# Identity made in place, and other places for transposes and value loads in a hybrid attention layer

## Chip, core and metric

The kernel runs on one core of one Trainium2 chip. Its time is the device time of one execution in microseconds. The program is one launch that computes the whole layer for two request groups.

## What is computed

One encoder layer with two parallel attentions, for two sequences (prompt and sample) of 2048 tokens and width 1024, all in fp32:

```python
h = rms_norm(x, norm_w)
q_a, k_a, v_a, g_a, q_b, k_b, v_b, g_b = jnp.split(h @ w_in, IN_SPLITS, axis=-1)
o_a = windowed_gqa_sink(rope(norm(q_a)), rope(norm(k_a)), v_a, sink_a) * jax.nn.silu(g_a)
o_b = neighbourhood_attn(norm(q_b), norm(k_b), v_b, rpb_b) * jax.nn.silu(g_b)
x = x + jnp.concatenate([o_a, o_b], axis=-1) @ w_out
out = x + (p @ w_ple) * jax.nn.sigmoid(x @ w_ple_gate)
```

The first attention has 8 query heads and 2 key heads and sees 128 tokens to each side. The second has 8 heads; it takes the tokens as a grid of 32 rows by 64 columns, and each token sees 8 rows by 16 columns around it, with a learned bias by relative position. The softmax of the second attention is over all keys that a query sees.

## The kernel before

**Products in split halves.** An fp32 operand is split into a high half (a cast to fp32r by ScalarE, ACT) and a low half (raw minus high, by VectorE, DVE). A product is then the sum of three fp32r products (high by high, high by low, low by high); `project` issues them, 8 blocks of 128 rows, so 24 matmuls for one output of 128 tokens by 512 columns.

**Units and filler.** The work is counted in tiles of 128 tokens, f from 0 to 95. f 0 to 31 are the first attention; f 32 to 95 are the second: 32 tiles for heads 0 to 3, then 32 for heads 4 to 7. A unit of the second attention (`unit_b`) takes one tile of queries, 8 grid rows by 16 columns, and a window of keys of 12 or 15 rows by 24 or 32 columns. The keys are cut into 3 or 4 chunks of at most 128 (`chunks`); 4 where the window is 15 rows by 32 columns. While a unit runs, TensorE also works through a stream of filler: the projections of later tiles (`proj_a`, `proj_b`) and, at the end, the first products of the gate branch (`ple_ahead`: pple, evicted as ev and stored to ple_d). The tables `PLAN_A` and `PLAN_B` say when each act of a unit comes, as a share of the tile's filler (the first number): all four "sc", then "exp", "prep" (the next unit's queries), "pt" and "po"; the entries with 0 in second place belong to the unit before ("po" 2 and 3, "fin"). A tile of filler is 10320, counted as 48 matmuls of 215 each; in the last units (`TAIL`) it is 8100. Whether a unit takes the one or the other table is decided in the last loop of `emit`.

**The acts of a unit of the second attention.** "sc" h makes the scores of head h in PSUM (scb) and VectorE adds the bias into s, with the row maximum (line 277); "exp" are four exponentials on ACT (line 301, order of heads 0, 2, 1, 3), which begin as soon as the maximum is negated into nm (line 295). "pt" x transposes the weights of the x-th head of that order to ptb, chunk by chunk; ACT and VectorE split it into p_t (lines 941 and 942). "po" x multiplies p_t by the values vw (pob); "fin" multiplies by the gate (o_tb) and stores to ob_d (line 970).

**Two kinds of units.** In most units, those for which `copied_(f)` is true (all but f 55 to 58 and 87 to 95, so 51 of 64), ACT also issues a DMA after each exponential that copies s, as it is, to a tile tn of type fp32r (line 310); the first copy goes out behind the second exponential, the second behind the third, the last two behind the fourth. Their transposes read tn and are line 262 in the trace. In the other 13 units, called fp32 units below, s is transposed itself (line 264).

**Value loads.** `load_values` issues the loads of vw, one for each chunk, on SP's queue (line 907). In a copied unit they are made to wait for one of the last four exponentials: `last_ex[1]`, which is the unit's second. SP's queue is in order, and most transfers stand on it: the blocks of x (stx), bias, the stores v_d and ob_d, and the reloads of split weights.

**Who sets the order.** TensorE's order is the program's, by dependencies that `pinned` adds. On the other engines a scheduler places instructions by when it takes their inputs to be ready, save those pinned with `P`. The queues run in the order in which they were placed. PSUM has buffers of three tags: "pj" (3, projections), "sc" (3, scores and transposes), "ms" (2, pob and others).

**The start.** The identity is made by GpSimd in a small pool of its own (`eye_`), cast by VectorE to `ident` and, with its columns in another order, by GpSimd to `rowwise`. The pool is closed at once, so its memory may be given to tiles that come later. Then come eight warm-up matmuls (pwarm), the loads of x blocks (stx) and weights (ws, wg), their splits (wx for keys and values of the first attention, wa for queries, wb for gates), and the first products: pk for tiles 0 and 1, then pq for both, then pg.

Of the kernel before, what the change touches and what calls it, by code (L numbers as in the profile page):

```python
# [11 lines left out]
F32 = mybir.dt.float32  # L12
F32R = mybir.dt.float32r
# [6 lines left out]
NT = SEQ // 128  # L20
# [38 lines left out]
def bias_offsets():  # L59
# [33 lines left out]
PLAN_A = (  # L93
    (0.04, 1, "sc", 0), (0.10, 1, "sc", 1), (0.12, 1, "sc", 2), (0.12, 1, "rest", 0), (0.14, 1, "sc", 3),
    (0.14, 1, "rest", 1), (0.14, 0, "po", 0),
    (0.22, 0, "po", 1), (0.34, 0, "po", 2), (0.45, 0, "fin", 0), (0.46, 1, "prep", 0), (0.58, 1, "den", 0),
    (0.75, 1, "pt", 0), (0.79, 1, "pt", 1), (0.88, 1, "pt", 2),
)
PLAN_B = (
    (0.00, 1, "sc", 0), (0.03, 1, "sc", 1), (0.07, 1, "sc", 2), (0.09, 0, "po", 2), (0.11, 1, "sc", 3), (0.16, 0, "po", 3),  # L100
    (0.16, 1, "exp", 0), (0.24, 0, "fin", 0), (0.35, 1, "prep", 0),
    (0.60, 1, "pt", 0), (0.68, 1, "pt", 1), (0.76, 1, "pt", 2), (0.91, 1, "po", 0), (0.94, 1, "pt", 3), (0.98, 1, "po", 1),
)


def emit(ctx, tc, io):
    nc = tc.nc
    dram = ctx.enter_context(tc.tile_pool(name="dram", bufs=1, space=bass.MemoryType.DRAM))
    cp = ctx.enter_context(tc.tile_pool(name="const", bufs=1))
# [3 lines left out]
        tag = PSM.get(tag, tag)  # L113
        return pp.tile(shape, F32, tag=tag, name=name, bufs=PSB[tag])

    ident, rowwise = (cp.tile([128, 128], F32R, tag=n, name=n) for n in ("ident", "rowwise"))
    with tc.tile_pool(name="eye", bufs=1) as ep:
        eye_ = ep.tile([128, 128], F32, tag="eye", name="eye")
        make_identity(nc, eye_)
        nc.vector.tensor_copy(ident, eye_)  # L120
        nc.gpsimd.tensor_copy(rowwise.rearrange("p (r c) -> p r c", c=16), eye_.rearrange("p (c r) -> p r c", r=8))
    nw = cp.tile([128, KT], F32, tag="nw", name="nw")
    nc.scalar.dma_start(nw, io["norm_w"])
    ms_a = cp.tile([128, 2 * NT], F32, tag="ms_a", name="ms_a")
# [159 lines left out]
    last_ex = []  # L284

    def after(ins, other):

        tc.add_manual_dep(ins.ins, other.name, mybir.DependencyInfo(mybir.DependencyClass.Sync, mybir.DependencyReason.DATA),
                          reason="behind the copies")
# [486 lines left out]
    def keys_b(kt, b, cb):  # L776
        pkt = ptile([128, 2, 16, 8], "ms", "pktb")
        for i in range(2):
            tr(pkt[:, i].rearrange("p c r -> p (c r)"), kt[:, 2 * i:2 * i + 2, :].rearrange("p h d -> p (h d)"))
        for e in range(2):  # L780
            a, z = 64 * e, 64 - 64 * e
            hi, lo = (ks_b[e][p:p + 64, 8 * b:8 * b + 8, :, 16 * cb:16 * cb + 16].rearrange("p r i c -> p i c r")
                      for p in (a, z))
            nc.scalar.copy(hi, pkt[a:a + 64])
            nc.vector.tensor_tensor(out=lo, in0=pkt[a:a + 64], in1=hi.bitcast(F32), op=ALU.subtract)
# [85 lines left out]

    bt = []

    def copied_(f):

        return not (4 * NT - 9 <= f < 4 * NT - 5 or f >= 6 * NT - 9)

    def unit_b(f):
        half, st = divmod(f - 2 * NT, 2 * NT)
        s, j = divmod(st, NT)  # L880
# [5 lines left out]
        n = nr * ncol  # L886
        if cb != 2:
            off, _ = BIAS_OFF[(row_type(b), col_type(cb))]
            if not bt:
                bt.append(big([128, 2, 4, 512], F32, "bias"))  # L890
            bt.append(bt[0][:, len(bt) % 2])
            load = nc.sync.dma_start(bt[-1][:, :, :n],
                                     io["bias"][half][:, off:off + 4 * n].rearrange("p (h n) -> p h n", h=4))
            if f > 2 * NT and copied_(f) and copied_(f - 1):
                after(load, last_ex[-1])
# [3 lines left out]
        def load_values():  # L899

            spare = f >= 6 * NT - 6 and f % 2 == 0
            if spare:
                four = ap.tile([128, 4, 4, 2 * HD], F32R, tag="raw", name="vw4", bufs=1)
            for j in range(nch):
                v = four[:, j] if spare else \
                    ap.tile([128, 4, 2 * HD], F32R, tag=("vp", "vr_")[j % 2], name="vw", bufs=3 - j % 2)
                load = nc.sync.dma_start(v[:kn[j]].bitcast(F32).rearrange("p h d -> p (h d)"),
                                         v_d[half, s, cb][r0 + ch[j][0]:r0 + sum(ch[j])]
                                         .rearrange("r c h a d -> (r c) (h a d)"))
                if copied_(f):  # L910
                    after(load, last_ex[1])
                vw.append(v)

        sees = [query_rows(b, cb, j) for j in range(nch)]
# [4 lines left out]
        def sc(h):  # L919
            ps = ptile([128, 512], "sc", "scb")  # L920
            for j, q in enumerate(qs[f]):
                mm(ps[:, :n].rearrange("p (r c) -> p r c", c=ncol), q[h % 2][:, 128 * (h // 2):128 * (h // 2) + 128],
                   ks_b[h % 2][:, r0:r0 + nr, h // 2, c0:c0 + ncol], j == 0, j == 1)
            softmax(h, ps, n, bias[:, h, :n], sm)
            if h == 3:
                if not tn:
                    tn.append(ap.tile([128, 4, 480], F32R, tag="ev", name="tn", bufs=1))
                got["ex"] = exps(sm, hr_b[:, st:st + 1], gs, turned=tn[0] if copied_(f) else None)
                next(got["ex"])
# [33 lines left out]
        def fin(_):  # L963
            pgt = ptile([128, 2, 128], "sc", "pgtb")
            for i in range(2):
# [4 lines left out]
            nc.sync.dma_start(ob_d[s][b, :, 2 * half:2 * half + 2, cb, :], o_t)  # L970
        return {"sc": sc, "pt": pt, "po": po, "fin": fin, "prep": lambda _: nxt(f),
                "exp": lambda _: (next(got["ex"]), load_values())}


# [106 lines left out]
    def drain(gen, count=10 ** 9):  # L1081
        for _ in range(count):
            if next(gen, None) is None:
                return
# [49 lines left out]
    for f in range(6 * NT):  # L1134
        in_a = f < 2 * NT
        while done < f + (2 if in_a else 6) and done < 6 * NT:
            drain(stream, 48 - owed)
            owed = 0
            done += 1
        total = 13008 if done < 2 * NT - 1 else 15480 if done < 2 * NT else 10320 if done < 6 * NT else TAIL  # L1140
        done += 1
        spent = 0
        for kv in range(2 if in_a else 1):
            unit = unit_a(f, kv) if in_a else unit_b(f)
            for part, now, act, i in PLAN_A if in_a else PLAN_B:
                at = (kv + part) / (2 if in_a else 1)
                while spent < at * total:
                    spent += next(stream, total)
                if now or prev:
                    (unit if now else prev)[act](i)  # L1150
            prev = unit
        while spent < total:
            spent += next(stream, total)
        if f in (2 * NT - 1, 6 * NT - 1):
            for part, now, act, i in PLAN_A if in_a else PLAN_B:
                if not now:
                    if f == 6 * NT - 1:
                        drain(stream, 4)
                    prev[act](i)
            prev = None  # L1160
        if f == 2 * NT - 1:
            for p in pending:
                drain(stream, 8)
                keys_b(*p)
            owed = 16
# [4 lines left out]
    with tc.tile_pool(name="c", bufs=1, reuse_waits="tile") as op:  # L1170
# [208 lines left out]
        for m in range(7 * len(groups)):  # L1379
            n, i = divmod(m, 7)  # L1380
# [94 lines left out]
```

## Time and profile before

| what | value |
|---|---|
| median of 3 runs | 2485.05 us (2482.97 to 2488.8) |
| profiled execution, its own time | 2484.0 us |
| its span, first to last instruction | 2482.2 us |
| mean granted clock of TensorE | 0.997 |
| TensorE busy | 2445.7 us (99%) |
| VectorE / ACT / GpSimd busy | 1699.0 / 1411.2 / 851.0 us |
| moved by DMA | 479.65 MB, mean 193 GB/s |

In rows of a timeline the first number is the start in us, the second the length; a row can stand for several instructions (x3), and the bracket tells how long the engine was idle before it and what ended that. PE is TensorE, PEld its weight loads, SPq and ACTq are the DMA issues of SP and ACT. In rows of waits the numbers are the total in us, how many times, and the longest. The profiled execution lies 1.05 us under the median, and 1.8 us of its time lie outside the span.

### The profile page before, as it was taken

Reading aid. Unit: us, or ns where it says so; the run is one execution under the profiler, and the core shown is the slowest. Engines: PE = TensorE matmul, PEld = TensorE weight load, DVE = VectorE, ACT = ScalarE, POOL = GpSimd, SP = SyncE. Lnnn points to the kernel's source line nnn. Section 1 sums busy time; section 2 is a strip of 40 time slices with the busy share of each in tenths; the row PEclk is TensorE's granted clock in tenths of the full one; section 3 lists DMA queues with packets and bytes.
Section 4 is the critical chain, followed back from the end, with each engine's and each line's share of the span. In section 5 each row is a group of like instructions: output and inputs, shape, how many; then the busy total and the mean of one; then the engine's idle time right before and its main releaser. Section 6 shows DMA issues by size and latency. Waiting matters only on the chain. (4 is left out here: it accounts for less than half of the span.)

```text
span 2482.2 us, 40847 instructions
## 1 busy us (share of the span) xinstructions
PE 2445.7 (99%) x13062; PEld 2063.1 (83%) x13062; DVE 1699.0 (68%) x4215; ACT 1411.2 (57%) x3408; POOL 851.0 (34%) x1363
## 2 busy tenths in 40 slices
PE   8999999999999999999999999999999999999999
PEld 7888888888888888887888788888788888888887
DVE  6877777777775666666666666666537655687776
ACT  6777777776754655665656566665663222344443
POOL 4555555555543544454544444443110000000000
PEclk9999999999999999999999999999999999999999
DMA  6422232322354667667966687778867455756765
GB/s 208 137 95 94 88 103 95 100 94 88 103 179 131 219 231 240 232 211 248 304 201 227 223 263 252 245 249 273 289 229 274 163 169 174 269 174 215 243 227 170
DMA packets 275255, 479.65 MB, mean 193 GB/s; under 512 B 31168, under 2 KB 116064, under 8 KB 270816
## 3 DMA queue, kind: packets, MB, share of 16 engines
q1 hardware_dynamic: 245376, 437.84, 53.4%
q10 hardware_dynamic: 29664, 39.19, 4.7%
q8 instruction: 104, 1.70, 0.3%
q14 instruction: 111, 0.91, 0.1%
HBM read 307.72 MB, written 134.23 MB: 178 GB/s over the span
## 5 line engine op out<-in xcount | busy, mean ns | idle before, releaser
L258 PE MATMUL pvg<-wb,xr 128*128 128x512 f32 x1536 | 447.8, 404 | 0.4 <-DMA wb<-sp_1wb 0.3
L258 PE MATMUL pqk<-wa,xr 128*128 128x512 f32 x1536 | 442.7, 411 | 0.0
L301 ACT ACTIVATE s<-s,nm 128x320 f32<-128x320 f32 (+6 forms) x512 | 293.2, 574 | 150.0 <-DVE nm L298 118.6
L258 PEld LDWEIGHTS pvg<-wb,xr 128*128 128x128 f32 x1536 | 270.4, 189 | 34.9 <-DMA wb<-sp_1wb 1.3
L258 PEld LDWEIGHTS pqk<-wa,xr 128*128 128x128 f32 x1536 | 262.1, 189 | 35.0
L1260 ACT CAST opd<-raw 128x512 fp32r<-128x512 f32 x224 | 131.5, 619 | 271.3 <-PE acca L1278 118.2
L379 POOL TENSOR_TENSOR xr<-stx,xr 128x512 fp32r<-128x512 f32 x186 | 237.6, 1293 | 117.4 <-ACT xr L378 91.3
L1261 DVE TENSOR_TENSOR opd<-raw,opd 128x512 fp32r<-128x512 f32 x224 | 146.5, 686 | 147.2 <-ACT opd L1260 147.2
L258 PE MATMUL pg<-wb,xr 128*128 128x512 f32 x768 | 233.1, 409 | 1.0 <-DVE vv L536 1.0
L258 PE MATMUL pq<-wa,xr 128*128 128x512 f32 x768 | 219.4, 400 | 0.0
L942 DVE TENSOR_TENSOR p_t<-ptb,p_t 128x368 fp32r<-128x368 f32 (+5 forms) x256 | 119.4, 486 | 125.9 <-ACT p_t L941 124.6
L941 ACT CAST p_t<-ptb 128x368 fp32r<-128x368 f32 (+5 forms) x256 | 106.8, 426 | 123.4 <-PE ptb L262 79.0
L1278 PE MATMUL accc<-opd,wb 128*128 128x512 f32 x768 | 176.7, 389 | 0.0
L1278 PE MATMUL acca<-opd,wa 128*128 128x512 f32 (+1 forms) x780 | 175.9, 386 | 0.5 <-ACT r L1356 0.5
L1278 PE MATMUL acca<-opd,s 128*128 128x512 f32 x768 | 175.4, 389 | 0.0
L1278 PEld LDWEIGHTS acca<-opd,wa 128*128 128x128 f32 x780 | 145.0, 188 | 30.2 <-ACT r L1356 0.7
L1278 PEld LDWEIGHTS accc<-opd,wb 128*128 128x128 f32 x768 | 144.2, 188 | 29.9
L1278 PEld LDWEIGHTS acca<-opd,s 128*128 128x128 f32 x768 | 144.2, 188 | 29.9
L960 ACT COPY otb<-pob 64x512 f32<-64x512 f32 x128 | 74.3, 581 | 160.1 <-PE pob L258 158.3
L143 POOL TENSOR_TENSOR yb<-vrb,power 128x8 f32<-128x8 f32 x64 | 106.4, 1662 | 148.7 <-DVE vrb L813 148.7
L258 PEld LDWEIGHTS pob<-p_t,vw 128*128 128x128 f32 (+2 forms) x832 | 134.2, 189 | 21.4 <-DVE p_t L942 1.5
L258 PEld LDWEIGHTS pq<-wa,xr 128*128 128x128 f32 x768 | 135.1, 189 | 17.3
(174 smaller groups left out, 5188.0 us busy)
## 6 DMA issues: line engine op xcount, KB each, us to landing
stx<-x_b SPq DMA_DIRECT2D x128, 256.0 KB
vw<-v_d SPq DMA_DIRECT2D x96, 256.0 KB
stx<-x_a SPq DMA_DIRECT2D x64, 256.0 KB
stn<-x_n SPq DMA_DIRECT2D x64, 256.0 KB
v_d<-vb SPq DMA_DIRECT2D x64, 256.0 KB
ple_d<-ev SPq DMA_DIRECT2D x64, 256.0 KB
xres<-x_r SPq DMA_DIRECT2D x64, 256.0 KB
x_d<-r SPq DMA_DIRECT2D x64, 256.0 KB
```

Source lines behind the costliest of these rows:

```text
L143: nc.gpsimd.tensor_tensor(out=y, in0=v, in1=power.broadcast_to([128, n]), op=ALU.pow)
L258: pinned(nc.tensor.matmul(out, lhsT, rhs, start=start, stop=stop))
L301: ex = nc.scalar.activation(ss[i], ss[i], AF.Exp, bias=nm[:, i:i + 1], accum_out=den[:, i:i + 1])
L379: low.tensor_tensor(out=lo, in0=raw, in1=hi.bitcast(F32), op=ALU.subtract)
L941: nc.scalar.copy(hi, pf)
L942: nc.vector.tensor_tensor(out=lo, in0=pf, in1=hi.bitcast(F32), op=ALU.subtract)
L960: nc.scalar.copy(ot[a:a + 64], pq[z:z + 64])
L1260: P(nc.scalar.copy(hi, v))
L1261: P(nc.vector.tensor_tensor(out=lo, in0=v, in1=hi.bitcast(F32), op=ALU.subtract))
L1278: pinned(nc.tensor.matmul(ps[:, cols], w[k][:, a, c:c + 128], o[:, b, cols], start=i in (0, 1, 4) and k == 0 and j == 0, stop=k == 3 and j ...
```

## The change

Three things change. The identity is made in `ident` itself, an fp32 tile, with no pool of its own and no cast; only `rowwise` is still a copy. `copied_` moves to the top and the fp32 units take `PLAN_B` with "pt" and "po" at 0.45 to 0.80 of the tile, the copied units a table `PLAN_C` of their own at 0.60 to 0.98. The value loads of copied units wait for `last_ex[2]`, the unit's third exponential.

```diff
 PLAN_B = (
     (0.00, 1, "sc", 0), ..., (0.16, 1, "exp", 0), (0.24, 0, "fin", 0), (0.35, 1, "prep", 0),
-    (0.60, 1, "pt", 0), (0.68, 1, "pt", 1), (0.76, 1, "pt", 2), (0.91, 1, "po", 0), (0.94, 1, "pt", 3), (0.98, 1, "po", 1),
+    (0.45, 1, "pt", 0), (0.52, 1, "pt", 1), (0.60, 1, "pt", 2), (0.66, 1, "po", 0), (0.74, 1, "pt", 3), (0.80, 1, "po", 1),
 )
+PLAN_C = (
+    (0.00, 1, "sc", 0), ..., (0.16, 1, "exp", 0), (0.24, 0, "fin", 0), (0.35, 1, "prep", 0),
+    (0.60, 1, "pt", 0), (0.70, 1, "pt", 1), (0.80, 1, "pt", 2), (0.92, 1, "po", 0), (0.95, 1, "pt", 3), (0.98, 1, "po", 1),
+)
+def copied_(f):
+
+    return 2 * NT <= f and not (4 * NT - 9 <= f < 4 * NT - 5 or f >= 6 * NT - 9)
...
-    ident, rowwise = (cp.tile([128, 128], F32R, tag=n, name=n) for n in ("ident", "rowwise"))
-    with tc.tile_pool(name="eye", bufs=1) as ep:
-        eye_ = ep.tile([128, 128], F32, tag="eye", name="eye")
-        make_identity(nc, eye_)
-        nc.vector.tensor_copy(ident, eye_)
-        nc.gpsimd.tensor_copy(rowwise.rearrange("p (r c) -> p r c", c=16), eye_.rearrange("p (c r) -> p r c", r=8))
+    ident = cp.tile([128, 128], F32, tag="ident", name="ident")
+    make_identity(nc, ident)
+
+    rowwise = cp.tile([128, 128], F32R, tag="rowwise", name="rowwise")
+    nc.gpsimd.tensor_copy(rowwise.rearrange("p (r c) -> p r c", c=16), ident.rearrange("p (c r) -> p r c", r=8))
...
                 if copied_(f):
-                    after(load, last_ex[1])
+                    after(load, last_ex[2])
...
-            for part, now, act, i in PLAN_A if in_a else PLAN_B:
+            for part, now, act, i in PLAN_A if in_a else PLAN_C if copied_(f) else PLAN_B:
```

What moves is seen in the engines' orders. First SP's queue at the very start of the program (stx are blocks of x, ws and wg raw weights: 128x2x256 those of pk, 128x2x512 those of pq; rw and snk_all are small tables), before:

```order
L238 DMA ws<-w_in 128x2x512 x2
L238 DMA wg<-w_in 128x512 x4
L433 DMA rw<-rope_w 128x64
L455 DMA snk_all<-sink 128x8
L361 DMA stx<-x_a 128x512
L238 DMA ws<-w_in 128x2x256
L361 DMA stx<-x_a 128x512
L238 DMA ws<-w_in 128x2x256 x3
```

and now:

```order
L370 DMA stx<-x_a 128x512
L247 DMA ws<-w_in 128x2x256
L370 DMA stx<-x_a 128x512
L247 DMA ws<-w_in 128x2x256 x3
L370 DMA stx<-x_a 128x512 x2
L247 DMA ws<-w_in 128x2x512 x4
L370 DMA stn<-x_n 128x512 x2
L247 DMA wg<-w_in 128x512 x4
L440 DMA cs<-rope 128x512
L442 DMA rw<-rope_w 128x64
L370 DMA stn<-x_n 128x512 x2
L464 DMA snk_all<-sink 128x8
```

The first block of x moves from the ninth transfer to the first, and the weights of pq and pg and the small tables go behind. VectorE's order there moves in the same way, before:

```order
L405 MEMSET warm 128x512
L120 CAST ident<-eye 128x128
L458 COPY snk<-snk_all 64x8 x2
L471 TENSOR_SCALAR snk<-snk 128x8
L158 SCALAR_TENSOR_TENSOR wa_113<-ws,nw,wa_113 128x512
```

and now:

```order
L414 MEMSET warm 128x512
L388 TENSOR_TENSOR xr<-stx,xr 128x512
L167 SCALAR_TENSOR_TENSOR wx<-ws,nw,wx 128x256 x2
L388 TENSOR_TENSOR xr<-stx,xr 128x512
L167 SCALAR_TENSOR_TENSOR wx<-ws,nw,wx 128x256 x6
```

The copy of the sink values (snk), which stood fourth, is now the 40th row.

Second, TensorE in a copied unit with four chunks (f = 37; pqk are the filler's matmuls, ptb the transposes), before:

```order
L262 MATMUL ptb<-rowwise,tn 128x128 x4
L258 MATMUL pqk<-wa_9503,xr 128x512
L258 MATMUL pqk<-wa_9505,xr 128x512 x3
L262 MATMUL ptb<-rowwise,tn 128x128 x4
L258 MATMUL pqk<-wa_9507,xr 128x512 x3
L258 MATMUL pqk<-wa_9509,xr 128x512
L262 MATMUL ptb<-rowwise,tn 128x128 x4
```

and now:

```order
L271 MATMUL ptb<-rowwise,tn 128x128 x4
L267 MATMUL pqk<-wa_9497,xr 128x512
L267 MATMUL pqk<-wa_9499,xr 128x512 x3
L267 MATMUL pqk<-wa_9501,xr 128x512
L271 MATMUL ptb<-rowwise,tn 128x128 x4
L267 MATMUL pqk<-wa_9501,xr 128x512 x2
L267 MATMUL pqk<-wa_9503,xr 128x512 x3
L271 MATMUL ptb<-rowwise,tn 128x128 x4
```

Five matmuls instead of four stand between the groups, so the second group comes one later and the third two; "po" 0 comes one later, and the fourth group stays. On SP's queue of the same stage the store of the tile before (ob_d) goes ahead of the value loads; before:

```order
L361 DMA stx<-x_b 128x512 x2
L907 DMA vw<-v_d_305 128x512 x3
L970 DMA ob_d_91<-o_tb 128x2x128
L846 DMA v_d_310<-vb 8x8x512
```

and now:

```order
L370 DMA stx<-x_b 128x512 x2
L975 DMA ob_d_85<-o_tb 128x2x128
L912 DMA vw<-v_d_299 128x512 x3
L855 DMA v_d_304<-vb 8x8x512
```

Third, ACT in an fp32 unit near the end (f = 91; ev evicts the filler pple, p_r splits its input, q1b are the next unit's queries, otb evicts pob), before:

```order
L866 ACTIVATE q1b<-pqtb,wk 64x256 x2
L1056 COPY ev<-pple 128x512 x2
L941 CAST p_t<-ptb 120x288 x2
L1056 COPY ev<-pple 128x512
L941 CAST p_t<-ptb 120x288
L994 CAST p_r<-p_22551 128x512
L1056 COPY ev<-pple 128x512
L994 CAST p_r<-p_22553 128x512
L941 CAST p_t<-ptb 120x288
L960 COPY otb<-pob 64x512
```

and now:

```order
L875 ACTIVATE q1b<-pqtb,wk 64x256
L946 CAST p_t<-ptb 120x288
L875 ACTIVATE q1b<-pqtb,wk 64x256
L1061 COPY ev<-pple 128x512
L946 CAST p_t<-ptb 120x288
L1061 COPY ev<-pple 128x512
L946 CAST p_t<-ptb 120x288 x2
L1061 COPY ev<-pple 128x512
L965 COPY otb<-pob 64x512
L1061 COPY ev<-pple 128x512
L999 CAST p_r<-p_22562 128x512
```

The first cast moves ahead of the second query cast, and the last of the four stands directly behind the third, ahead of both splits of p.

More of the change, by code (lines that the diff above doesn't have):

```diff
@@ L101 @@
     (0.16, 1, "exp", 0), (0.24, 0, "fin", 0), (0.35, 1, "prep", 0),
-    (0.60, 1, "pt", 0), (0.68, 1, "pt", 1), (0.76, 1, "pt", 2), (0.91, 1, "po", 0), (0.94, 1, "pt", 3), (0.98, 1, "po", 1),
+    (0.45, 1, "pt", 0), (0.52, 1, "pt", 1), (0.60, 1, "pt", 2), (0.66, 1, "po", 0), (0.74, 1, "pt", 3), (0.80, 1, "po", 1),
 )
+PLAN_C = (
+    (0.00, 1, "sc", 0), (0.03, 1, "sc", 1), (0.07, 1, "sc", 2), (0.09, 0, "po", 2), (0.11, 1, "sc", 3), (0.16, 0, "po", 3),
+    (0.16, 1, "exp", 0), (0.24, 0, "fin", 0), (0.35, 1, "prep", 0),
+    (0.60, 1, "pt", 0), (0.70, 1, "pt", 1), (0.80, 1, "pt", 2), (0.92, 1, "po", 0), (0.95, 1, "pt", 3), (0.98, 1, "po", 1),
+)
+def copied_(f):
+    return 2 * NT <= f and not (4 * NT - 9 <= f < 4 * NT - 5 or f >= 6 * NT - 9)
 def emit(ctx, tc, io):
@@ L872, in emit @@
     bt = []
-    def copied_(f):
-        return not (4 * NT - 9 <= f < 4 * NT - 5 or f >= 6 * NT - 9)
     def unit_b(f):
```

## Prediction

> **What bounds the kernel now.** I read the page's busy line first, then the list of waits of TensorE, then the timelines around its longest waits, and last the windows that show the clock.
>
> ```profile
> PE 2445.7 (99%) x13062; PEld 2063.1 (83%) x13062; DVE 1699.0 (68%) x4215; ACT 1411.2 (57%) x3408; POOL 851.0 (34%) x1363
> PE ptb L262 <- DMA tn<-s: 10.6, 16, 2.2
> PE pk L258 <- issue: 7.2, 1, 7.2
> PE scb L258 <- DVE p_t L942: 3.8, 1, 3.8
> ```
>
> TensorE is busy for 2445.7 of 2482.2 us. The change adds and removes no product (13,064 in the program, before and after), so all it can win lies in the 36.5 us in which TensorE stands still, and in time that it runs at half clock. Three entries make up most of the 36.5: the transposes of the second attention that wait for a copied tile, the start, and one wait of 3.8 us late in that stage. The change has a part at each of them.
>
> **Part 1, the start.** The rows are from the timelines of the first 32 us.
>
> ```profile
> 0.72 0.97 SPq L238 DMA_DIRECT2D ws<-w_in  x2
> 4.94 1.28 ACT L157 ACT_TABLE_LOAD   x1 [4.94 <-DMA ws<-w_in]
> 6.07 0.33 SPq L361 DMA_DIRECT2D stx<-x_a  x1
> 9.40 0.34 DVE L458 COPY snk<-snk_all 64x8 f32<-64x8 f32 x2 [6.92 <-DMA snk_all<-sink]
> 10.67 0.62 ACT L378 CAST xr<-stx 128x512 fp32r<-128x512 f32 x1 [3.10 <-DMA stx<-x_a]
> 12.41 0.55 PE L258 MATMUL pk<-wx,xr 128*128 128x256 f32 x1 [7.17 <-issue]
> 14.01 2.46 DVE L158 SCALAR_TENSOR_TENSOR wx<-ws,nw,wx 128x256 fp32r<-128x256 f32 x6
> 20.27 11.07 PE L258 MATMUL pq<-wa,xr 128*128 128x512 f32 x48
> 18.51 2.83 DVE L158 SCALAR_TENSOR_TENSOR wa<-ws,nw,wa 128x512 fp32r<-128x512 f32 x4
> 31.17 4.93 PE L258 MATMUL pg<-wb,xr 128*128 128x512 f32 x21
> ```
>
> The first product (pk) needs a block of x (stx) and the first weights (ws into wx). SP sends the block as its ninth transfer, at 6.07; ACT casts it at 10.67, 4.6 us later. VectorE meanwhile stands behind the copy of the sink values until 9.40. In the changed order SP's first transfer is that block, the second the weights of pk, and the sink copy stands behind three of the gate weights' low halves. Both parts follow from the identity: no pool of its own is closed ahead of the loads.
>
> When does pk start then? The first transfer of 512 KB, issued at 0.72, released ACT at 4.94. The block has 256 KB and the same place, so it lands by 4.9, I take 4.2 to 4.9. The cast takes 0.62, pk's first weights land one transfer later and cost another 0.4 on ACT (2.46/6 on VectorE). The table load (1.28) stood behind the landing; now it may run ahead of it or not. That gives 5.5 to 7.6 instead of 12.41: 4.8 to 6.9 us.
>
> Does the lead survive? VectorE must make the low halves: 4 blocks of x at 0.69, 8 of wx at 0.41, 8 of wa at 0.71, then 8 of wb.
>
> ```profile
> 5.25:12.41 7.16, 0.00 (x0) 0.03 (x1) 2.94 (x7) 4.05 (x7) 0.00 (x0) 0.79 1.01 329
> 12.41:20.27 7.86, 7.67 (x49) 7.34 (x50) 7.86 (x17) 7.47 (x16) 0.00 (x0) 0.76 1.02 342
> 9.40:31.17 21.77, 18.57 (x96) 16.38 (x97) 21.28 (x54) 17.93 (x38) 5.77 (x10) 0.84 0.89 304
> 28.16 2.73 DVE L158 SCALAR_TENSOR_TENSOR wb<-ws,nw,wb 128x512 fp32r<-128x512 f32 x4
> ```
>
> (Columns of the windows: length, busy time of PE, PEld, DVE, ACT and POOL, clock, DMA share, GB/s.) From 9.40 to 31.17 VectorE worked 21.28 of 21.77 us and TensorE only just found its data ready, the last wb at 30.9. If VectorE starts on x at about 5, its 21.3 us of work end at 26.3 at the earliest; some 3 us of waits (the transfers of 1 MB and more per 2.8 us, ACT's squares behind products) put the last wb near 29.7. TensorE reaches the second x block at about 10.3, needs 24 products of 256 columns for it (0.12 each, half of pq's 11.07/48 = 0.23), then the 48 of pq: 13.0 + 11.1 = 24.1 for the first pg, which is 7 us ahead of 31.17. Eight wb steps at the pace of VectorE then cost it 0.6: **6.3 us** stay. The lower bound is 4.8 from the first product, the upper 7.2, the whole idle window, plus 1.7 of half clock: between 12.41 and 20.27 the clock was 0.76 of 7.86 us, so 0.24 x 7.86 = 1.9 us less work done, nearly all of it hidden again if VectorE sets the pace.
>
> **Part 2, the copied units** (51 of the 64). Here a tile's exponentials go through a DMA (tn from s) before they are transposed.
>
> ```profile
> 1135.45 0.47 PE L262 MATMUL ptb<-rowwise,tn 128*120 128x128 f32 x3 [2.20 <-DMA tn<-s]
> 1257.63 0.44 PE L262 MATMUL ptb<-rowwise,tn 128*120 128x128 f32 x3 [1.47 <-DMA tn<-s]
> 1518.30 0.41 PE L262 MATMUL ptb<-rowwise,tn 128*120 128x128 f32 x3 [0.73 <-DMA tn<-s]
> PE ptb L262 <- DVE qg L850: 0.5, 1, 0.5
> PE ptb L262 <- DVE p_t L942: 0.4, 1, 0.4
> PE ptb L262 <- DVE ks_b L785: 0.3, 1, 0.3
> ```
>
> Going through the timeline, the 16 waits of 10.6 us are by group of transposes: first 3.2 (3 times, the longest at 1135.45), second 3.9 (4, the longest at 1257.63), third 3.3 (8, the longest at 1518.30), fourth 0.2 (1). In the order TensorE's second group moves back by one product of 0.23, the third by two (0.46), the first and fourth not at all, the first product with values (pob) by one. The loads of values move too. One unit shows how they stand to the copies:
>
> ```profile
> 1511.46 0.60 ACT L301 ACTIVATE s<-s,nm 128x360 f32<-128x360 f32 x1
> 1511.51 1.32 SPq L907 DMA_DIRECT2D vw<-v_d  x3
> 1511.56 0.50 ACTq L310 DMA_DIRECT2D tn<-s  x1
> 1511.77 0.42 DVE L969 TENSOR_TENSOR o_tb<-pgtb,o_tb 128x256 f32<-128x256 f32 x1 [0.39 <-POOL o_tb L968]
> 1512.21 0.51 ACTq L310 DMA_DIRECT2D tn<-s  x1
> 1512.93 0.58 SPq L970 DMA_DIRECT2D ob_d<-o_tb  x1
> vw<-v_d SPq DMA_DIRECT2D x96, 256.0 KB
> ```
>
> Today two of the three loads leave ahead of the third copy (1512.21). Behind the third exponential they could leave at 1512.1; but SP's order now also has the store of the tile before (ob_d) ahead of them, which waits for o_tb (1512.19) and takes 0.58. So they leave from 1512.8, 1.3 us later, after three of the four copies. 256 KB at the 329 to 342 GB/s of the windows above is 0.77 us. A copy that had up to two loads ahead of it gains 0 to 1.5; I take 0.35 for the second and 0.7 for the third (halves, since two queues share the engines). Then the third group's 3.3 is gone, the fourth's 0.2 too, the second keeps 0.87, 0.3 and 0.3 of its four (2.4 won), the first wins 0.4. The three waits put down to VectorE are in second and third groups; I count 1.0 of 1.2. Sum 7.3, less 0.3 for values that come late: **7 us**. Bounds: 11.8 if all of it goes, 2 if the shift alone helps and values take the rest back. The queues passed: ACT's casts of xr move one place ahead of the second p_t cast in some units, and SP's later loads stand 1.3 us longer behind the values; TensorE does not wait for either in the rows read.
>
> [...]
>
> **Part 3, the 13 fp32 units.** They transpose s itself. The last nine stand at the end of the stage.
>
> ```profile
> 1774.56 0.49 PE L264 MATMUL ptb<-rowwise,s 128*120 128x128 f32 x3
> 1778.63 0.58 ACT L1056 COPY ev<-pple 128x512 f32<-128x512 f32 x1 [4.05 <-DMA ple_d<-ev]
> 1779.63 0.40 ACT L941 CAST p_t<-ptb 120x288 fp32r<-120x288 f32 x1
> 1780.88 0.61 PE L258 MATMUL scb<-ks_b,q1b 128*128 128x288 f32 x1 [3.79 <-DVE p_t L942]
> 1780.80:1784.30 3.50, 3.42 (x11) 3.09 (x12) 2.27 (x11) 0.45 (x1) 0.00 (x0) 0.51 0.80 251
> ```
>
> The fourth transposes of a unit (1774.56) were cast only at 1779.63, because an eviction ahead of the cast waited 4.05 us for the store of its buffer; scores of the next unit needed that PSUM buffer. In the new order all four casts stand ahead of that eviction, so the 3.8 goes, and with it a stretch of 3.5 us at clock 0.51 (1.7 us). What is late next is the eviction itself: the projection's three buffers fill in two more groups of six products, about 4 us with what lies between, so 0 to 2 us of waiting come back. Two waits of values for p_t (1.1 us) at the stage's end go as well. Against this, casts have less room: the first values follow the first transposes after 0.21 instead of 0.31 of the tile.
>
> ```profile
> 1188.05 0.49 PE L264 MATMUL ptb<-rowwise,s 128*120 128x128 f32 x3
> 1190.48 0.40 ACT L941 CAST p_t<-ptb 120x288 fp32r<-120x288 f32 x1
> 1192.52 0.47 PE L258 MATMUL pob<-p_t,vw 120*128 120x256 f32 x3
> ```
>
> Today this cast comes 2.4 us after its transposes, without harm. The best is 6.6 won (3.8 + 1.7 + 1.1); the worst 2 lost by new waits on casts. I take **3 us**, since the order brings the casts forward with the transposes.
>
> [...]
>
> **Sum.** The profiled execution took 2484.0 us (span 2482.2): 2484.0 - 6.3 - 7 - 3 = 2467.7. The median of the runs is 1.05 above it, so **2469 us**.
>
> **Rivals.**
> - Values become what is late. If po waits in the 12 copied units with four chunks, for the 1.3 us less the one product (0.23), that is up to 12 us; about half, 6, is my price: 2475. For: the rows of pob have one wait for values already (below), so some unit has no slack. Against: that is the only one. 17%.
>
> ```profile
>   DMA vw<-v_d: 0.2, 1
> ```
>
> - The start is set by VectorE and ACT alone: a square behind pq delays wb's casts and 3 us of the 6.3 come back: 2472. For: 21.28 of 21.77 us busy. 12%.
> - Only the start helps: transfers land as before, the late stall moves to the eviction: 2484.0 - 6.3 + 1 = 2479. 8%.
> - Slower: the casts of the fp32 units do not follow. The first values would stand at 1189.7 in the unit above (0.25 of 10.3 us earlier, with the products' own pace), and the low half is done at 1190.48 + 0.40 + 0.5 = 1191.4: 1.7 us in each of 13 units, 22 us, against 13 won: 2494. It decides once casts lag by over 2.3 us after the change. Against: the first cast now stands right behind the first query cast, ahead of the eviction. 5%.
>
> **How the numbers follow.** The forecast has 58%. Its own bounds (head 4.8 to 8.9, part 2 from 2 to 11.8, part 3 from -2 to 6.6) end at 2458 and 2480; with the rivals that leaves the range at 2459 to 2480. About 0.2%, 5 us, is what can be told from no change: faster than 2480 has 0.87, the same 0.08, slower 0.05.
>
> **What would show it.** Right: the first pk near 6 and the first pg near 24 to 25; ptb's waits on tn at 2 to 5 us and no third group among them; no wait of 3.8 near 1770. Wrong: rows "pob <- DMA vw" above 2 us in sum, "pob <- DVE p_t" in the units at 1175 to 1230, or a pg that starts after 27.

## The result, and the profile after

The changed kernel takes 2469.36 us in the median of 4 runs (2466.96 to 2471.02), the kernel before 2484.31 us (2482.97 to 2488.8, 4 runs). The ratio is 0.9936 with a 95% interval of 0.9919 to 0.9953: 16 us faster (12 to 20). The forecast was 2469. In a second comparison (experiment 5 below) the ratio was 0.9928 (0.9915 to 0.9940), 18 us, so the gain is given as 16 to 18 us here.

The profiled execution took 2468.76 us (span 2466.9). The busy line and TensorE's list of waits, in us in total, times, and the longest:

```profile
PE 2443.6 (99%) x13062; PEld 2065.4 (84%) x13062; DVE 1702.1 (69%) x4214; ACT 1412.6 (57%) x3408; POOL 852.9 (35%) x1363
PE ptb L271 <- DMA tn<-s: 6.8, 4, 2.9
PE pob L267 <- DMA vw<-v_d: 3.3, 8, 1.1
PE scb L267 <- DVE mx L286: 2.1, 1, 2.1
```

TensorE does the same work; its idle time fell from 36.5 to 23.3 us. The wait of the first pk is gone. The waits on tn are 4 instead of 16, but still 6.8 us. Two entries are new or have changed their name: values (vw) are waited for 8 times, and the scores late in the stage wait 2.1 us for a row maximum instead of 3.8 us for p_t.

The start, from the timeline of the changed kernel (the second pk, of tile 2, is the last row):

```profile
1.65 1.28 ACT L387 ACT_TABLE_LOAD   x1 [1.65 <-PEq L1472]
3.76 0.62 ACT L387 CAST xr<-stx 128x512 fp32r<-128x512 f32 x1 [0.83 <-DMA stx<-x_a]
5.49 8.44 PE L267 MATMUL pk<-wx,xr 128*128 128x256 f32 x48 [0.24 <-ACT wx L166]
13.77 11.07 PE L267 MATMUL pq<-wa,xr 128*128 128x512 f32 x48
24.68 4.97 PE L267 MATMUL pg<-wb,xr 128*128 128x512 f32 x21
26.71 2.73 DVE L167 SCALAR_TENSOR_TENSOR wb<-ws,nw,wb 128x512 fp32r<-128x512 f32 x4
36.72 3.03 PE L267 MATMUL pk<-wx,xr 128*128 128x256 f32 x24
```

and, of the kernel before, the same pk and the next wait; then one window of the changed kernel (length, busy time of PE, PEld, DVE, ACT and POOL, clock, DMA share, GB/s):

```profile
42.82 3.04 PE L258 MATMUL pk<-wx,xr 128*128 128x256 f32 x24
48.47 0.51 PE L258 MATMUL sc<-ks_a,q 128*128 128x256 f32 x2 [0.77 <-DVE mx L277]
```

```profile
5.49:13.77 8.28, 8.28 (x48) 7.81 (x49) 7.33 (x14) 7.19 (x15) 0.00 (x0) 1.00 1.03 376
```

The first pk is 6.92 us earlier, the first pg 6.49, the second pk 6.10; then the 0.77 us wait of the scores does not come back, and from there the lead is 7.2 us. The clock in pk is 1.00 instead of 0.76, and yet its 48 products take 8.28 us instead of 7.86: they run at the pace of their data (VectorE 7.33 and ACT 7.19 of 8.28 us busy, DMA share 1.03), so the full clock won nothing that shows there.

The waits in the copied units that matter:

```profile
1126.78 0.44 PE L271 MATMUL ptb<-rowwise,tn 128*120 128x128 f32 x3 [1.87 <-DMA tn<-s]
1165.76 0.44 PE L267 MATMUL pob<-p_t,vw 128*128 128x128 f32 x2 [0.52 <-DMA vw<-v_d]
1401.23 0.53 PE L271 MATMUL ptb<-rowwise,tn 128*128 128x128 f32 x4 [1.91 <-DMA tn<-s]
1645.10 0.56 PE L271 MATMUL ptb<-rowwise,tn 128*120 128x128 f32 x3 [2.88 <-DMA tn<-s]
1686.19 0.44 PE L267 MATMUL pob<-p_t,vw 128*128 128x128 f32 x2 [1.05 <-DMA vw<-v_d]
```

All four tn waits are in first groups (f = 52, 69, 84 and 86); no second, third or fourth group waits. Two of the waits, those of 1.91 and 2.88 us, were followed by 3.41 us at half clock each (0.50 from 1402.87 to 1406.28 and from 1645.22 to 1648.63; five products of pqk took 2.46 us in the first of them, 1.39 us just before it), by an estimate about 1.7 us more each time (half of 3.41). And the end of the stage:

```profile
1767.23 0.59 ACT L1061 COPY ev<-pple 128x512 f32<-128x512 f32 x1 [3.01 <-DMA ple_d<-ev]
1767.84 1.14 ACT L999 CAST p_r<-p 128x512 fp32r<-128x512 f32 x2
1768.49 0.69 DVE L1000 TENSOR_TENSOR p_r<-p,p_r 128x512 fp32r<-128x512 f32 x1 [3.55 <-DMA wb<-sp_oa]
1769.62 0.40 PE L267 MATMUL scb<-ks_b,q1b 128*128 128x288 f32 x1 [2.11 <-DVE mx L286]
```

The eviction still waits for its store, 3.01 us. The casts are ahead of it now, but the split of p stands behind it on ACT, its low half ahead of the score adds on VectorE, and the scores need a PSUM buffer that those adds free. (The row names a transfer of wb as releaser of the low half; but the low half began 0.65 us into the two casts of p_r on ACT, when the first was done.) The chain is longer by two links, the wait shorter by 1.7 us.

If one matches the products of the two traces by their place in the order, the lead is 7.2 us when the second attention starts (a pqk at 750.10 before, 742.93 after), 9.4 us at the first pple, and 15.2 us from the end of that stage on. By this pair of traces alone the start is worth 7.2, the copied units with the first four fp32 units 2.2, the last units 5.8. The experiments show how far such a reading can be trusted.

### The profile page after: what moved, and what is told of

It is laid out like the page before. It is cut to its first block, busy times and chain, and to the rows that moved or that the text cites. A ratio compares the mean times of both kernels' runs of the same rounds, so it can differ in the third digit from the quotient of the medians.

```text
span 2466.9 us, 40869 instructions
## 1 busy us (share of the span) xinstructions
PE 2443.6 (99%) x13062; PEld 2065.4 (84%) x13062; DVE 1702.1 (69%) x4214; ACT 1412.6 (57%) x3408; POOL 852.9 (35%) x1363
## 4 chain that ended last, share of the span: by engine, by line
PE 90%; DMA 4%; DVE 3%; ACT 2%; issue 1%; POOL 1%; SPq 0%; ACTq 0%; DVEq 0%; POOLq 0%
PE acca L1283 14%; PE pvg L267 14%; PE pqk L267 13%; PE accc L1283 11%; PE pq L267 6%; PE pg L267 6%; PE scb L267 4%; PE pob L267 3%; PE pk L267 3%; PE pple L267 3%; PE po L267 3%; PE sc L267 3%; PE pt L273 2%; DMA vw<-v_d 2%; PE ptb L271 2%; DMA tn<-s 1%
```

## The experiments

Each was timed against the kernel before on the same chip; "us under before" is the ratio times 2483 us, with the ends of its interval in brackets. Experiments 1 to 4 ran on one chip, 5 to 8 on a second and 9 to 12 on a third, so medians in us are compared within such a group only, and across groups by the ratios. Kernel 3 is the kernel of experiment 3, and so on.

A list of waits is of one execution, and that one is not always typical: in experiments 3, 4 and 6 it is among the fastest (2473.41 us where the median is 2477.05, 2472.94 for 2479.45, 2461.62 for 2464.81), in experiment 10 it is the slowest (2476.12 for 2470.85).

**1. The identity alone** (on the kernel before).

```diff
-    ident, rowwise = (cp.tile([128, 128], F32R, tag=n, name=n) for n in ("ident", "rowwise"))
-    with tc.tile_pool(name="eye", bufs=1) as ep:
...
+    ident = cp.tile([128, 128], F32, tag="ident", name="ident")
+    make_identity(nc, ident)
...
```

> The kernel before with the identity made in place, and nothing else. The prediction's first part: 6.3 us faster (bounds 4.8 to 8.9). What the changed kernel's trace suggests instead: 7.2 us, because the second block of first products (pk) starts 6.1 us earlier and the wait of 0.77 us of the scores at 48.47 us goes as well. Under both the first pk starts near 5.5, the first pg near 24.7 us, and the second attention shows the waits of before: 8 to 12 us on tn, one wait of 3 to 4 us near 1770. If the start is not additive with the rest, the gain differs from the 7.2 us by which the changed kernel is ahead at 700 us.

Measured: ratio 0.9960 (0.9947 to 0.9974), 9.9 us under before (6.5 to 13.2). Its trace is 7.3 us ahead at the first pk and 8.6 us at the start of the second attention. In the ten traces with the new identity that lead, against the one trace of before, was 6.7 to 8.6 us (8.0 in the mean); in the three without it, -0.5 to 1.0 (0.2). So the start is worth about 7.8 us, and what goes beyond that in the 9.9 lies within the interval.

**2. The fp32 units' table alone.**

```diff
-    (0.60, 1, "pt", 0), (0.68, 1, "pt", 1), (0.76, 1, "pt", 2), (0.91, 1, "po", 0), ...
+    (0.45, 1, "pt", 0), (0.52, 1, "pt", 1), (0.60, 1, "pt", 2), (0.66, 1, "po", 0), ...
```

This is the table as the fp32 units see it; the copied units keep the old one under another name.

> The kernel before with only the 13 fp32 units on the new table (pt and po at 0.45 to 0.80); copied units, values and identity as before. The prediction's third part: 3 us faster (-2 to 6.6), the 3.8 us wait gone and up to 2 us of it back at the evictions. The rival from the changed kernel's trace: 5.5 to 6 us faster, nearly all of it after 1740 us (the stretch at half clock and the three waits of pple on ev go as well), with one wait of about 2 us left at the scores near 1785. If it shows under 4 us, the 5.9 us that the changed kernel won at its end came partly from somewhere else.

Measured: 0.9986 (0.9975 to 0.9996), 3.5 us under before (1.0 to 6.2). The wait of the scores is 3.5 us and put down to mx, as in the changed kernel; the three waits of pple on ev are gone.

**3. The copied units' table alone.**

```diff
-    (0.60, 1, "pt", 0), (0.68, 1, "pt", 1), (0.76, 1, "pt", 2), (0.91, 1, "po", 0), (0.94, 1, "pt", 3), ...
+    (0.60, 1, "pt", 0), (0.70, 1, "pt", 1), (0.80, 1, "pt", 2), (0.92, 1, "po", 0), (0.95, 1, "pt", 3), ...
```

This is the table as the copied units see it; the fp32 units keep the old one.

> The kernel before with only the 51 copied units on the new table (second group of transposes one product later, third two, first values one); value loads behind the second exponential as before. If the shift alone hides the copies: waits on tn fall from 10.6 to about 6 us (first groups stay at 3.2, second lose 0.23 each, third lose 0.46 each) and the time by 4 to 5 us; no wait on values. If the loads of values are what holds the copies up, third groups keep their waits and it is 2 us or less.

Measured: 0.9975 (0.9965 to 0.9985), 6.2 us under before (3.7 to 8.7). The waits on tn fell to 6.0 us (11 times), as the shift alone was expected to do, and one wait on values (0.7) appeared.

**4. The values alone.**

```diff
-                    after(load, last_ex[1])
+                    after(load, last_ex[2])
```

> The kernel before with only the value loads behind the third exponential. By the prediction the second and third copies land 0.35 to 0.7 us sooner, waits on tn fall to 4 to 6 us, values cost 0.3: 3 to 5 us faster. By the rival (what the copies gain the values lose) waits of pob on vw add up to 3 to 6 us, since po 0 stands one product earlier here than in the changed kernel, and the time stays within 2 us of before, or is longer.

Measured: 0.9984 (0.9975 to 0.9992), 4.0 us under before (2.0 to 6.2). Its list of waits:

```profile
PE pob L258 <- DMA vw<-v_d: 3.9, 9, 0.7
PE ptb L262 <- DMA tn<-s: 1.5, 3, 0.7
```

In this execution, the fastest of its 12, the copies' waits nearly vanish, and the values give 3.9 us of it back in 9 places. Both theories had one half right. The four parts alone add up to 23.6 us, the whole change wins 16 to 18. With 2 to 3.4 us of uncertainty on each part the difference could be chance, but it suggests that two of them are after the same waits.

**5. The changed kernel once more**, as a yardstick.

> The changed kernel itself once more, as the yardstick of the next three and to see which of its waits return. If the three long waits of first transposes on tn (1.87 at 1126.78, 1.91 at 1401.23, 2.88 at 1645.10) come from the order of the transfers, they stand again at f = 52, 69 and 84 with 1 us or more each; if they are chance, two of the three are under 0.7 us or elsewhere. Waits of pob on vw: 2 to 5 us in 6 to 10 places. Time 12 to 20 us under before.

Measured: 2464.95 us, 0.9928 (0.9915 to 0.9940), 17.9 us under before. Its waits:

```profile
PE pob L267 <- DMA vw<-v_d: 4.1, 9, 0.8
PE scb L267 <- DVE mx L286: 4.0, 1, 4.0
PE ptb L271 <- DMA tn<-s: 1.7, 2, 0.9
```

The long first waits of f = 52 and 84 did not return (their first copies landed 4.7 us after the maximum, against 7.6 and 8.6 in the first trace); that of f = 69 did, with 0.9 in the first and 0.8 in the second group. The wait of the scores was 4.0 instead of 2.1. By this trace the start is worth 7.6, the copied stage 8.8, the last units 2.6 us, where the first gave 7.2, 2.2 and 5.8. Same program: how much a stage waits on transfers differs by several us from one execution to the next, so a term of 3 us cannot be read from one pair of traces. The two stretches at half clock after the waits of the first trace have no like in the copied stage of the second, which makes about 3.4 us of the difference there.

**6. The changed kernel with its values early again.**

```diff
-                    after(load, last_ex[2])
+                    after(load, last_ex[1])
```

> The changed kernel with the value loads behind the second exponential again (last_ex[1]). If the moved transposes do the work and the moved loads only trade one wait for another: waits of pob on vw fall from 3.3 to under 1 us, waits of transposes on tn in second and third groups come back with 2 to 4 us, and the time is within 2 us of the changed kernel. If the later loads are worth the 3 us or more that they showed alone, this is 3 us or more slower than the changed kernel.

Measured: 2464.81 us, 0.9923 (0.9910 to 0.9935), no different from the changed kernel beside it (2464.95).

```profile
PE ptb L271 <- DMA tn<-s: 3.6, 8, 0.9
PE pob L267 <- DMA vw<-v_d: 0.6, 1, 0.6
```

So with the transposes moved, the later loads are worth nothing that shows (the ratios differ by 0.0005, with an uncertainty of some 0.0018): 3.6 + 0.6 us of waits here, 1.7 + 4.1 there. That the loads won 4.0 us alone, in experiment 4, fits this if they were after the same waits as the moved transposes of experiment 3. The time from the start of the negation of the maximum to the end of each transfer, averaged over the 51 copied units, shows the exchange:

| kernel | copies 1, 2, 3, 4 (us) | values: first, last (us) |
|---|---|---|
| before | 3.97, 6.22, 7.90, 9.16 | 5.42, 8.53 |
| changed, first trace | 3.98, 4.82, 6.17, 8.07 | 7.13, 9.59 |
| changed, second trace | 3.82, 4.72, 6.16, 7.93 | 7.04, 9.51 |
| values early (6) | 3.87, 6.06, 7.79, 9.03 | 5.29, 8.43 |
| bias and store later (8) | 3.71, 4.64, 6.68, 8.36 | 5.94, 8.89 |

**7. Four bias loads behind the copies.** In the first trace of the changed kernel a load of bias for an fp32 unit, which waits for no exponential, goes out just ahead of the copies of f = 84:

```profile
1636.49 0.38 SPq L897 DMA_DIRECT2D bias<-bias  x1
1638.00 0.47 ACTq L319 DMA_DIRECT2D tn<-s  x1
bias<-bias SPq DMA_DIRECT2D x16, 720.0 KB
```

```diff
             if f > 2 * NT and copied_(f) and copied_(f - 1):
                 after(load, last_ex[-1])
+            elif f in BEHIND:
+                after(load, ends[f - BEHIND[f]])
...
```

`BEHIND` tells how many units back to look (f 55: 3, 56: 2, 87: 3, 88: 2), and `ends` holds the fourth exponential of each unit; the lines that fill them are left out here.

> The changed kernel with four loads of bias (those of the fp32 units f = 55, 56, 87 and 88, which wait for no exponential and go out just ahead of the copies of f = 52, 54, 84 and 86) made to wait for the fourth exponential of f = 52, 54, 84 and 86. If these 720 KB loads are what holds the first copies of f = 52 and 84 up: the first transposes of these two units wait under 0.7 us, and the time is 2 to 5 us under the changed kernel. If the backlog has another source, the waits stay and the time is within 1.5 us; if the bias then comes late itself, waits of scores or longer tiles near 1170 and 1690 show it.

Measured: 2461.22 us, 0.9912 (0.9898 to 0.9925), 3.7 us under the changed kernel in the medians; the two ratios' intervals overlap, but all five runs (2459.93 to 2462.63) lie under the five of the changed kernel beside them (2463.09 to 2467.40). The first copies of f = 52, 54, 84 and 86 landed 0.5 to 1.1 us sooner than in the second trace of the changed kernel, and 1.0 to 1.4 us sooner in experiment 8 than in 9, which differ by this edit alone. So the loads do hold these copies up, by about 1 us; the 3 to 5 us of the first trace they do not explain. Nor does it show where the 3.7 us come from, since beside it only f = 69 had waited for a copy.

**8. The store behind the fourth exponential as well.**

```diff
-            nc.sync.dma_start(ob_d[s][b, :, 2 * half:2 * half + 2, cb, :], o_t)
+            store = nc.sync.dma_start(ob_d[s][b, :, 2 * half:2 * half + 2, cb, :], o_t)
+            if copied_(f) and copied_(f + 1):
+                after(store, last_ex[-1])
```

> As the one before, and in copied units the store of the tile before (ob_d) also waits for the fourth exponential, so that SP's queue sends the value loads ahead of it. If values come late because they stand behind this store (1.25 us after the third exponential), waits of pob on vw fall from 3.3 to about 1 us and the time is 1 to 3 us under the kernel with the bias loads moved alone. If the engines' backlog sets when values land, vw waits stay at 2 us or more, or second and third copies wait again, and the time stays within 1 us.

Measured: 2455.52 us, 0.9889 (0.9875 to 0.9902), 27.6 us under before (24.3 to 31.0) and 9.4 us under the changed kernel, the fastest of all but for kernel 12, which equals it. It is 5.7 us under experiment 7, where 1 to 3 were expected. The same tile (f = 75) in the changed kernel and in this one, third exponential, store and values:

```profile
1499.32 0.60 ACT L310 ACTIVATE s<-s,nm 128x360 f32<-128x360 f32 x1
1500.09 0.38 SPq L975 DMA_DIRECT2D ob_d<-o_tb  x1
1500.57 1.50 SPq L912 DMA_DIRECT2D vw<-v_d  x3
```

```profile
1491.12 0.60 ACT L310 ACTIVATE s<-s,nm 128x360 f32<-128x360 f32 x1
1491.83 1.30 SPq L915 DMA_DIRECT2D vw<-v_d  x3
1493.26 0.54 SPq L978 DMA_DIRECT2D ob_d<-o_tb  x1
```

In the changed kernel the values leave 0.65 us after the third exponential, here 0.11 us. They land 1.1 to 1.2 us (first) and 0.6 to 0.7 us (last) sooner (table), the second copies keep their gain, the third and fourth give back 0.5 and 0.3 to 0.4, and the list of waits has no row on vw, where experiment 7 still had 2.7 us, and one on tn:

```profile
PE ptb L271 <- DMA tn<-s: 0.2, 1, 0.2
```

Most of what the copies gained is had without the price: it is the store that gives way, and TensorE's list has no wait for it. Some 1.3 us of the 5.7 are a shorter wait of the scores near 1755 (2.0 instead of 3.3), which the store is not shown to cause.

**9. The store alone.** The edit of 8 without that of 7.

> The changed kernel with only the store of the tile before (ob_d) behind the fourth exponential in copied units; the bias loads as in the changed kernel. If the store alone holds the values up (loads at 3.3 instead of 2.1 us after the maximum), waits of pob on vw fall from about 4 to under 1 us here too and this has 6 us of the 9.4 us that both edits won: 2457 to 2460. If the bias loads matter as much, first transposes of f = 52 and 84 wait again, and it is 3 us or more over the kernel with both edits.

Measured: 2459.03 us, 0.9906 (0.9892 to 0.9920): 23.3 us under before. Waits on vw 1.1 us (3 times), on tn 1.7 (2 times), so the store has about 5 of the 9 to 10 us and the bias loads the rest, though the step between the two kernels (0.0017) is about as large as its uncertainty.

**10. The changed kernel without part 2** (copied units on the old table, values behind `last_ex[1]`).

> The changed kernel without part 2: the copied units on the old table and their values behind the second exponential; the identity and the fp32 units' table stay. By the prediction's sum part 2 is worth 7 us, so this is 9 us under before and 7 us over the changed kernel (2465 on the last chip). By the changed kernel's first trace (3 us net) it is 3 us over it. If the parts together win less than each alone (identity 11, fp32 units 4, copied table 6, values 3 us under before), this comes to 13 to 15 us under before, within 4 us of the changed kernel.

Measured: 2470.85 us, 0.9955 (0.9942 to 0.9968), 11.2 us under before. Beside the changed kernel's 0.9928 and 0.9936 part 2 is worth 5 to 7 us, with some 5 us of uncertainty; none of the three expected figures (7 and 3 us over the changed kernel, or 13 to 15 under before) is ruled out. Its trace, of the slowest run, has the old waits: 11.3 us on tn in 17 places, 0.3 on vw.

**11. The changed kernel without part 3** (fp32 units on the old table).

> The changed kernel without part 3: the fp32 units on the old table. By the prediction it loses 3 us against the changed kernel, by that kernel's first trace 5.9 us, by the run of the fp32 table alone 3.5. The wait of the scores near 1765 is put down to p_t again with 2 to 4 us, and the two or three waits of pple on ev (1.1 us) are back.

Measured: 2469.61 us, 0.9946 (0.9934 to 0.9959), 13.4 us under before. Part 3 is worth 2.5 to 4.5 us by this, with the same uncertainty, about what it was alone (3.5); the 5.8 of the first pair of traces is above all three, though not ruled out. The wait of the scores is 4.2 us and put down to p_t again, and 1.1 us of pple on ev is back, as expected.

**12. The low half of p on GpSimd**, on top of 8.

```diff
             nc.scalar.copy(hi, src)
-            nc.vector.tensor_tensor(out=lo, in0=src, in1=hi.bitcast(F32), op=ALU.subtract)
+            (nc.vector if later else nc.gpsimd).tensor_tensor(out=lo, in0=src, in1=hi.bitcast(F32), op=ALU.subtract)
```

> The kernel with both edits (bias and store later), and the low half of the splits of p in the last units on GpSimd, which does little there, instead of VectorE. If the 2 us wait of the scores near 1755 comes from the score adds standing behind that split on VectorE, which waits for ACT behind an eviction, it goes, and the time is 1 to 3 us under 2455.5. If the eviction's wait for its store (2.9 us) holds TensorE by its own buffers, a wait of pple on ev takes its place, and the time is the same.

Measured: 2454.92 us, 0.9887 (0.9871 to 0.9903), the same as 8 (0.9889). The wait of the scores is gone, and others stand in its place:

```profile
1755.49 0.59 ACT L1066 COPY ev<-pple 128x512 f32<-128x512 f32 x1 [4.56 <-DMA ple_d<-ev]
1756.12 0.73 PE L267 MATMUL pple<-p_r,wa 128*128 128x512 f32 x2 [0.62 <-ACT ev L1066]
1759.56 0.53 PE L273 MATMUL ptb<-rowwise,s 128*96 128x128 f32 x3 [0.64 <-ACT s L310]
1776.88 0.56 PE L267 MATMUL pob<-p_t,vw 128*128 128x256 f32 x3 [0.48 <-DVE p_t L950]
```

The eviction waits 4.56 us for its store here (2.9 at most in experiment 8); what stands behind it on ACT is late, whichever engine makes the low half. This points at that store as what bounds the place, but earlier stores or more buffers for ev were not tried.

## Why the prediction was right, and where it was not

The sum was right: 16.3 us forecast, 16 to 18 measured. Not every term was, and that they make up for each other is partly luck. Term by term:

**Part 1 (6.3 forecast, about 7.8 measured).** The first pk was put at 5.5 to 7.6 and started at 5.49; the block landed at about 3.8, under the 4.2 to 4.9 taken, and the table load was over by 2.93 us, ahead of it. The last wb was put at 29.7 and ended at 29.44, the first pg at 24.1 and came at 24.68. The second pk kept 6.1 of the 6.5 us that the first pg had won, so the loss put behind it (0.6) was about right. What the prediction lacked is the 0.77 us wait of the scores at 48.47, which went as well. The rival that VectorE and ACT give 3 us of this back did not happen. Experiment 1 shows that the new way to make the identity is the cause; whether it is the pool or the cast that is gone was not tried apart.

**Part 2 (7 forecast, 5 to 7 measured).** The total is right, two of its steps are mis-sized. "I take 0.35 for the second and 0.7 for the third": the table has 1.4 and 1.7 us. "0.3 for values that come late": 3.3 and 4.1 us in the two traces. The first error is in the halves: the copies gained about all of the 1.5 us that the prediction gave as the most, not half of it. The second is in the slack. The loads left 1.2 us later (1.3 forecast) and landed 1.7 (first) and 1.1 us (last) later, about as the prediction had it, but it priced this at 0.3 without a row for how long the products with values could wait. In experiment 6 the two nearly cancel. The place of the price was seen (the loads go out behind the store of the tile before), its size was left to the first rival, which put 6 us on it. The prediction's own sign for "wrong", rows of pob on vw above 2 us, came true. The three waits put down to VectorE are gone in both traces, as counted. That the total came out right all the same is luck: kernel 6, which has the moved transposes without the later loads, is as fast, so the transposes alone seem to win what the forecast gave to both. The page gives the packet time of both queues as a share of the core's 16 DMA engines; in the kernel before (packets, MB, share; by the bytes issued, q1 is SP's queue, with the value loads, and q10 is ACT's, with the copies):

```profile
q1 hardware_dynamic: 245376, 437.84, 53.4%
q10 hardware_dynamic: 29664, 39.19, 4.7%
```

The table of experiment 6 shows the exchange: later loads, sooner copies, and 1.4 and 1.7 us gained for 1.1 to 1.7 lost. Experiment 8 shows that a later store lets both be in time (no wait on vw, 0.2 us on tn).

First groups: "the first wins 0.4" is not settled. They waited 3.2 us before, 6.8 and 0.9 in the two traces of the changed kernel. At f = 69 a wait of 0.2 to 2.1 us in all stood in every trace (in that of 6 in the third group); three transfers of 1.5 MB together (a store of sums of 1 MB and two blocks of x) leave there 6 to 10 us before the first copy, but no experiment moved them.

**Part 3 (3 forecast, 2.5 to 4.5 measured).** "The 3.8 goes" failed as told: what went is its name. In its place stood 2.1 and 4.0 us on mx, at the upper bound of the "0 to 2 us" of waiting that was put on the eviction, and over it. The 1.7 us of half clock counted behind the 3.8 went in the first trace (full clock after 2.1 us) and stood again in the second, where about 3.4 us at half clock follow the 4.0 (four windows of 1 us from 1765.46 on at 0.51, 0.50, 0.50 and 0.78). Won were the 1.1 us of pple on ev and half of the 1.1 us of pob on p_t. The rival that the fp32 units' casts lag did not happen. In f = 56 the first cast runs 1.1 us after its transposes instead of 2.4, and the first values follow without a wait:

```profile
1191.22 0.49 PE L273 MATMUL ptb<-rowwise,s 128*120 128x128 f32 x3
1192.31 0.40 ACT L946 CAST p_t<-ptb 120x288 fp32r<-120x288 f32 x1
1194.54 0.47 PE L267 MATMUL pob<-p_t,vw 120*128 120x256 f32 x3
```

## What to carry to other kernels

Where later loads come with sooner copies, as here (values 1.1 to 1.7 us later, second and third copies 1.4 and 1.7 us sooner), delaying one group of transfers can just move the wait to the other; look for a third transfer on the same queue that nobody is waiting for (here a store ahead of the loads: with it and four bias loads later, waits on vw and tn fell from the 4.1 and 1.7 us of the second trace of the changed kernel to none and 0.2) and delay that one. Parts of a change that are after the same wait do not add: each alone may look worth it, and leaving one out of the whole shows whether it is. A term of a few us in a stage that waits for transfers is read from several executions or from timed variants, not from one pair of traces.

## What was not expected of the hardware

Half clock does not follow the length of a wait alone. The prediction let a stretch at clock 0.51 go with the wait of 3.79 us ahead of it. But the changed kernel's clock fell after 1.91 us of waiting that ended at 1401.23, and in kernel 3 a wait of 3.32 us was followed by full clock:

```profile
1403.00:1404.00 1.00, 1.00 (x6) 0.90 (x5) 0.97 (x2) 0.98 (x3) 0.22 (x1) 0.50 0.85 249
```

```profile
1771.61 0.40 PE L268 MATMUL scb<-ks_b,q1b 128*128 128x288 f32 x1 [3.32 <-DVE p_t L948]
1771.61:1774.61 3.00, 3.00 (x18) 2.64 (x19) 2.27 (x10) 1.01 (x4) 0.00 (x0) 1.00 0.85 283
```

In the changed kernel's trace the two stretches at 0.50 lasted 3.41 us each and came behind waits of 1.91 and 2.88 us, while the clock was 1.00 for as long behind those of 1.87 us (ended at 1126.78) and 2.11 us (at 1769.62). In the trace of the kernel before it was 0.50 for 3.41 us from 1135.74 and from 1780.86, behind waits of 2.20 and 3.79 us. What decides whether half clock follows a wait was not shown, so a wait's length alone does not tell what half clock adds to it.

The same program also spreads by several us between executions on one chip: kernel 4 ran from 2472.94 to 2482.78 us in 12 runs, the kernel before from 2475.61 to 2486.12 in 27.
